# Padding of SBUF to multiples of 512 bytes, and another spread of the modulation row sums, in a two-block kernel on one core

## The chip, the core and the metric

The kernel runs on one core of a Trainium2 chip. Its time is the device time of one execution, in microseconds: 1427.51 us, the median of 3 runs (1427.47 to 1428.04). All data of a core pass through SBUF, a memory of 128 partitions in which a tile has a start address in bytes, the same in each partition. TensorE multiplies a stationary operand of 128 by 128 values, which a weight load brings in, with a moving operand of up to 512 columns that streams past it; both lie in SBUF.

## The reference

Two blocks are computed one after the other for 256 tokens of width 1024; the second also has 256 context tokens. All is float32. Cut to what matters here:

```python
# first block
x = x + 0.5 * swiglu(rmsnorm(x, ffn1_norm), gate, up, down)      # 1024 -> 2816 -> 1024
x = x + hybrid_mixer(rmsnorm(x, mix_norm), ...)                   # gated linear attention, conv
x = x + 0.5 * swiglu(rmsnorm(x, ffn2_norm), gate, up, down)
x = rmsnorm(x, final_norm)
# second block
h, hc = x + grid_pos_emb, ctx
mods   = split(silu(c)     @ w_ada + b_ada, 9)                    # w_ada: 1024 x 9216
mods_c = split(silu(c_ctx) @ w_ada + b_ada, 9)
h  = h  + 0.5 * mods[2]   * swiglu(modulate(rmsnorm(h),  mods[0],   mods[1]))
hc = hc + 0.5 * mods_c[2] * swiglu(modulate(rmsnorm(hc), mods_c[0], mods_c[1]))
h  = h + mods[5] * mixer(modulate(rmsnorm(h), mods[3], mods[4]), same of hc with mods_c)
h  = h + 0.5 * mods[8] * swiglu(modulate(rmsnorm(h), mods[6], mods[7]))
out = rmsnorm(h, g_final)
```

`modulate(x, shift, scale)` is `x * (1 + scale) + shift`.

## The kernel before, in words

**Products.** Each float32 product is made of three matmuls in the type fp32r. Every operand is held as a high and a low part: ScalarE writes the high part (`split_out`, line 66's activation, tiles `wh`, `XH`), VectorE the rest (line 69's subtraction, tiles `wl`, `XL`), and `mm3`, `mm3r`, `projT` and `projT2` add high by high, high by low and low by high into one PSUM tile `acc`. The matmul itself is line 79 for all of them.

**Stages.** The first block has a gated feed-forward layer for 256 tokens (`ffn2tok`: the gate-up projection in 11 steps of 4 units, then the down projection `d1` in 22 units), a mixer, and a second such layer (`ffn2tok` with `mid`, the preparation of the second block's inputs). The second block has a feed-forward layer for all 512 tokens (`ffn4tok`, two parts with a gate-up and a down projection each; a down projection runs twice, for either half of the 1024 outputs, over four tiles of 128 tokens), a mixer, and a last layer for 256 tokens.

**Units.** Weights come in units of 128 by 1024 values, 512 KB. SP's queue loads a unit into one of 4 buffers `raw`, ScalarE and VectorE split it into one of 5 pairs `wh`, `wl`. Units are handled in the order in which the code is written; each engine works its queue in order.

**Which operand is which.** In `proj_chunk` and in the down projections the weights stream (`wh`, `wl`, 512 columns of 4 bytes) past activations that are loaded as stationary operand: 128-column pieces of `XH` and `XL`, or of the tiles `S0` to `S17` that hold the hidden layer's high and low parts. In `projT2` the weights are stationary and `XH`, `XL` stream, 512 or 256 columns wide.

**Addresses.** Tiles are laid out one after the other, each rounded up to 32 bytes. What begins where, as the sizes of the tiles give it (bytes, and the rest after division by 512):

| tile | before: first byte | rest | after: first byte | rest |
|---|---|---|---|---|
| `ident` | 16512 | 128 | 16896 | 0 |
| `XH` | 18080 | 160 | 17408 | 0 |
| `XL` | 34464 | 160 | 33792 | 0 |
| `S0` | 91776 | 128 | 92672 | 0 |
| `S1` | 95904 | 160 | 97280 | 0 |
| `S2`, `S3` | 100032, 104128 | 192 | 101888, 105984 | 0 |
| `S4` to `S7` | 108256 + 4096 n | 224 | 110592 + 4096 n | 0 |
| `S8` to `S12` | 124672 + 4096 n | 256 | 127488 + 4096 n | 0 |
| `S13` to `S17` | 145184 + 4096 n | 288 | 148480 + 4096 n | 0 |
| `raw` (4), `wh` (5), `wl` (5) | 165664 + 4096 n | 288 | 168960 + 4096 n | 0 |

The rests of the `S` tiles differ because five of them once hold rows of 1032 values (4128 bytes; `CU` and `VH`), 32 bytes more than the others. Pieces of an operand lie at multiples of 512 bytes from its tile's start in nearly all products (exceptions: `VH`, with rows of 1032 bytes, and the second piece of `w_qk`, 1088 bytes in).

**Row sums.** `ada_gen` computes the modulation vectors `mods` outside TensorE: for each of 72 units of `w_ada` it loads the unit into a `raw` buffer and has VectorE multiply it with the broadcast silu(c) and sum each row (line 543; twice, for c and c_ctx, in the first 40 units, once in the last 32). It is a generator: `split` runs one more step of it after every `fill_every`-th unit of weights. `mid` runs it until 24 steps are done, `prep` to its end.

Of the kernel before, what the change touches and what calls it, by code (L numbers as in the profile page):

```python
# [9 lines left out]
F32 = mybir.dt.float32  # L10
F32R = mybir.dt.float32r
# [3 lines left out]
P = 128  # L15
D = 1024
FF = 2816
NF = FF // P
# [5 lines left out]
class Kern:  # L24
# [26 lines left out]
    def psum(self, tag, shape):  # L51
        return self.ps.tile(shape, F32, tag=tag, name=self.nm(tag), bufs=4)

    def salloc(self, shape, dt=F32):
        i = self.free_slots.pop(0)
        t = self.slots.tile(shape, dt, tag=f"S{i}", name=self.nm(f"S{i}"))
        self.slot_of[id(t)] = (i, t)
        return t

# [261 lines left out]
    def ffn2tok(self, Wgu, Wd, xts, rows, sink, after, skew=4, cols=False, first_by_tile=False, w0=(), fine=False, mid=None, ahead=None):  # L321


        hT = {}

        def dest(f):
            g = f // 4
            if g not in hT:
                hT[g] = (self.salloc([P, 4, 256], F32R), self.salloc([P, 4, 256], F32R))
            return hT[g] + (f % 4,)  # L330

        for c in range(1 if cols else 11):
            self.fill_every = 2 if self.filler is not None and 1 <= c < 10 else 0
            trs = []

            def sink_gu(t, ps, c=c, trs=trs):
                i = [a for a, _ in xts].index(t)
                r = rows.get(t)
                sil = self.t2([P, 256])
                h = self.t2([P, 256])  # L340
                if r is None:
                    self.act(sil, ps[:, :256], AF.Silu)
                    self.tt(h, ps[:, 256:], sil, ALU.mult)
                else:
                    self.act(sil, ps[:, :256], AF.Silu, scale=r)
                    self.stt(h, ps[:, 256:], r, sil, ALU.mult, ALU.mult)

                def later():
                    if i == 0:
                        trs.append(self.psum("tr", [P, 2, 256]))  # L350
                    tr = trs[0]
                    for f in range(2):
                        self.nc.tensor.transpose(tr[:, f, i * P:i * P + P], h[:, f * P:f * P + P], self.ident)
                    if i == 1:
                        hh, hl, sl = dest(2 * c)
                        self.split_out(hh[:, sl:sl + 2, :], hl[:, sl:sl + 2, :], tr)

                self.defer(later)

            self.proj_chunk(Wgu, 4 * c, xts, sink_gu, flush_at=2, last_by_tile=c == 0 and first_by_tile)  # L360
            if c == 0 and w0:
                for w in w0:
                    self.sfree(*w)
                self.held = 3
        if cols:
            toks = slice(xts[0][0] * P, xts[0][0] * P + 256)
            for f in range(2, NF):
                self.fill_every = 3 if self.filler is not None and f < 20 else 0
                ws = [self.unit(Wgu[2 * f + j]) for j in range(2)]
                pss = [self.psum("acc", [P, 256]) for _ in range(2)]  # L370
                self.projT2(pss, ws, toks)
                sil, h = self.t2([P, 256]), self.t2([P, 256])
                self.act(sil, pss[0], AF.Silu)
                self.tt(h, pss[1], sil, ALU.mult)
                hh, hl, sl = dest(f)
                self.split_out(hh[:, sl, :], hl[:, sl, :], h)
                if f == 2:
                    self.flush()
        if mid is not None:
            mid()  # L380
        ps = {}

        def step(f, i, t, d, w):
            wh, wl = w
            hh, hl, sl = dest(f)
            s = slice(d * 512, d * 512 + 512)
            if f == 0:
                ps[t, d] = self.psum("acc", [P, 512])
            a, b = hh[:, sl, i * P:i * P + P], hl[:, sl, i * P:i * P + P]
            self.mm3(ps[t, d], a, b, wh[:, s], wl[:, s], f == 0, f == NF - 1)  # L390

        for f in range(NF - skew):
            wh, wl = self.unit(Wd[f])
            hh, hl, sl = dest(f)
            groups = []
            for i, (t, _) in enumerate(xts):
                for d in range(2):
                    s = slice(d * 512, d * 512 + 512)
                    if f == 0:
                        ps[t, d] = self.psum("acc", [P, 512])  # L400
                    a, b = hh[:, sl, i * P:i * P + P], hl[:, sl, i * P:i * P + P]
                    groups.append((ps[t, d], a, b, wh[:, s], wl[:, s]))
            if fine and f == NF - skew - 1:
                self.mm3r(groups[:3], False, False)
                self.mm3r(groups[3:], False, True)
                sink(t, d, ps[t, d])
                continue
            for q in (groups[:2], groups[2:]) if f == 0 else (groups,):
                self.mm3r(q, f == 0, False)
            if f == 0:  # L410
                self.flush()
        ws = [self.unit(Wd[f]) for f in range(NF - skew, NF)]
        if ahead is not None:
            for g in range((NF - skew) // 4):
                self.sfree(*hT.pop(g))
            ahead()
        for i, (t, _) in enumerate(xts):
            for d in range(2):
                if fine and i == 1 and d == 1:
                    for q in (slice(0, 384), slice(384, 512)):  # L420
                        pq = self.psum("tr", [P, q.stop - q.start])
                        for f in range(NF - skew, NF):
                            (wh, wl), (hh, hl, sl) = ws[f - NF + skew], dest(f)
                            w = slice(512 + q.start, 512 + q.stop)
                            a, b = hh[:, sl, i * P:i * P + P], hl[:, sl, i * P:i * P + P]
                            self.mm3(pq, a, b, wh[:, w], wl[:, w], f == NF - skew, f == NF - 1)
                        sink(t, d, pq, q)
                        after(t, d, q)
                    continue
                for f in range(NF - skew, NF):  # L430
                    step(f, i, t, d, ws[f - NF + skew])
                sink(t, d, ps[t, d])
                after(t, d)
        for a, b in hT.values():
            self.sfree(a, b)

    def ffn4tok(self, Wgu, Wd, xts, sink, after, ws):

        u0 = 0
        for part, (f0, f1) in enumerate(((0, 12), (12, 22))):  # L440
# [15 lines left out]
            f = f0  # L456
# [12 lines left out]
            for f in range(f, f1):  # L469
# [2 lines left out]
                pss = [self.psum("acc", [P, 512]) for _ in range(2)]  # L472
                self.projT2(pss, ws, slice(0, 512))
                sink_gu(f, *pss)
            self.fill_every = 0
            nu = (f1 - f0) // 2
            for d in range(2):
                pss = {}

                def step(u, i, t, w):  # L480
# [623 lines left out]
    def run(self):  # L1104
        nc, A = self.nc, self.A
        x = {}
        for t in (2, 3):
            x[t] = self.xres.tile([P, D], F32, tag=f"x{t}", name=f"x{t}")
        self.ident = self.cpool.tile([P, P], F32, tag="ident", name="ident")
        make_identity(nc, self.ident)  # L1110
        g = {"f1": self.bc.tile([P, D], F32, tag="bc", name="bc_f1")}
        pre = []
# [5 lines left out]
        self.mhalf = self.cpool.tile([P, 4], F32, tag="mhalf", name="mhalf")  # L1118
        nc.gpsimd.memset(self.mhalf, -0.5)
        self.tri = self.cpool.tile([P, 2, P], F32, tag="tri", name="tri")  # L1120
        self.XH = self.cpool.tile([P, 8, 512], F32R, tag="XH", name="XH")
        self.XL = self.cpool.tile([P, 8, 512], F32R, tag="XL", name="XL")
        lat = (2, 3)

        def res_half(t, d, ps):
# [173 lines left out]
def body(tc, A, out):  # L1299
    with tc.tile_pool(name="const", bufs=1) as cpool, \  # L1300
            tc.tile_pool(name="xres", bufs=1) as xres, \
            tc.tile_pool(name="small", bufs=16) as small, \
            tc.tile_pool(name="tmp", bufs=6) as tmp, \
            tc.tile_pool(name="bc", bufs=4) as bc, \
            tc.tile_pool(name="rp", bufs=2) as rp, \
            tc.tile_pool(name="slots", bufs=1) as slots, \
            tc.tile_pool(name="raw", bufs=4) as raw, \
            tc.tile_pool(name="wsp", bufs=5) as wsp, \
            tc.tile_pool(name="dram", bufs=1, space=bass.MemoryType.DRAM) as dram, \
            tc.tile_pool(name="ps", bufs=1, space=bass.MemoryType.PSUM) as ps:  # L1310
        pools = dict(cpool=cpool, xres=xres, small=small, tmp=tmp, bc=bc, rp=rp, slots=slots, raw=raw, wsp=wsp, ps=ps)
        k = Kern(tc, A, out, pools)
        k.modd = dram.tile([112, P], F32, tag="modd", name="modd")
        k.mrow = dram.tile([36, 256], F32, tag="mrow", name="mrow")
        k.run()
# [129 lines left out]
```

## Time and profile before

| | us |
|---|---|
| median of 3 runs | 1427.51 |
| the profiled execution | 1426.11 |
| its span, first to last instruction | 1424.3 |
| TensorE busy in the span | 1404.2 (99%) |
| VectorE busy | 919.5 (65%) |
| ScalarE busy | 626.5 (44%) |

The page's sections are read from the top: busy time by engine, the span in 40 slices, DMA queues, the chain that ended last, groups of instructions. Matmuls overlap in the profile (the next begins before the last is out), so a group's mean duration is not its cost; the cost of one is the distance from one start to the next, and that is a stretch's length by its count of weight loads (one per matmul) in the view of busy time by stretch.

### The profile page before, as it was taken

The page shows a single profiled execution, that of the slowest core. Times are in us where ns is not written, and L with a number is a line of the kernel's source. Part 1 is how long each engine was busy: PE and PEld are TensorE (multiplying, and loading weights), DVE is VectorE, ACT ScalarE, POOL GpSimd, SP SyncE. Part 2 cuts the span into 40 slices and gives each one's busy share as a digit, 9 for nine tenths or more (in the row PEclk, how much of TensorE's full clock was granted, in tenths as well). Part 3 has the DMA queues.
Part 4 walks back from the last instruction along what each step waited for, and adds up shares of the span by engine and source line. Part 5 has one row for each costly group of instructions (what it writes and reads, how often), then busy time and mean ns, then how long its engine had stood idle before and what let it go on. Part 6 is the DMA issues. An engine that isn't in the chain of part 4 may idle for free. (4 is left out here: it accounts for less than half of the span.)

```text
span 1424.3 us, 18795 instructions
## 1 busy us (share of the span) xinstructions
PE 1404.2 (99%) x7222; PEld 1170.0 (82%) x7222; DVE 919.5 (65%) x1308; ACT 626.5 (44%) x914; POOL 29.3 (2%) x49
## 2 busy tenths in 40 slices
PE   7999999999999999999999999999999999999997
PEld 5888788778888898888888887888988887899986
DVE  5998556878988475542555446476886566655545
ACT  5445447464446442322122224343865455444442
POOL 0000000000000000000000001001010000000000
PEclk9999999999999999999999999999999999999999
DMA  8888646457887664643565442333335666465662
GB/s 278 307 269 275 205 136 204 134 166 259 290 275 254 203 210 132 195 147 102 191 209 178 147 148 94 115 104 129 102 104 187 198 192 206 142 197 179 184 207 69
DMA packets 73307, 260.71 MB, mean 183 GB/s; under 512 B 8172, under 2 KB 9216, under 8 KB 73216
## 3 DMA queue, kind: packets, MB, share of 16 engines
q1 hardware_dynamic: 72928, 259.11, 56.3%
q8 instruction: 57, 0.93, 0.3%
q10 hardware_dynamic: 288, 0.39, 0.1%
q14 instruction: 34, 0.28, 0.1%
HBM read 258.32 MB, written 1.14 MB: 182 GB/s over the span
## 5 line engine op out<-in xcount | busy, mean ns | idle before, releaser
L69 DVE TENSOR_TENSOR wl<-raw,wh 128x1024 fp32r<-128x1024 f32 (+1 forms) x381 | 459.0, 1212 | 330.3 <-ACT wh L66 326.7
L66 ACT ACTIVATE wh<-raw 128x1024 fp32r<-128x1024 f32 (+1 forms) x381 | 398.3, 1049 | 609.0 <-PE acc L79 457.9
L79 PE MATMUL acc<-wh,XH 128*128 128x512 f32 (+2 forms) x816 | 277.3, 398 | 0.4 <-ACT t L66 0.4
L79 PE MATMUL acc<-wh,XL 128*128 128x512 f32 (+2 forms) x816 | 273.4, 393 | 0.2 <-DVE XL L69 0.2
L79 PE MATMUL acc<-wl,XH 128*128 128x512 f32 (+2 forms) x816 | 272.4, 392 | 0.0
L79 PE MATMUL acc<-wh,S 128*128 128x512 f32 x872 | 237.1, 394 | 0.4 <-DVE t L72 0.4
L79 PE MATMUL acc<-XH,wh 128*128 128x512 f32 (+1 forms) x776 | 201.5, 339 | 0.0
L79 PE MATMUL acc<-XH,wl 128*128 128x512 f32 (+1 forms) x776 | 201.2, 339 | 0.0
L79 PE MATMUL acc<-XL,wh 128*128 128x512 f32 (+1 forms) x776 | 201.1, 339 | 0.0
L79 PEld LDWEIGHTS acc<-wh,S 128*128 128x128 f32 x872 | 162.8, 188 | 38.8 <-DVE t L72 1.1
L543 DVE SCALAR_TENSOR_TENSOR S<-raw,S 128x1024 f32<-128x1024 f32 x112 | 136.9, 1222 | 70.6 <-DMA raw<-in_w_ada 69.9
L79 PEld LDWEIGHTS acc<-wh,XL 128*128 128x128 f32 x816 | 152.2, 189 | 34.6 <-DVE XL L69 1.1
L79 PEld LDWEIGHTS acc<-wl,XH 128*128 128x128 f32 x816 | 152.0, 188 | 33.7 <-DVE wl L69 0.3
L79 PEld LDWEIGHTS acc<-wh,XH 128*128 128x128 f32 x816 | 151.7, 189 | 33.9 <-ACT t L66 0.6
L79 PEld LDWEIGHTS acc<-XL,wh 128*128 128x128 f32 x776 | 133.0, 188 | 17.5
L79 PEld LDWEIGHTS acc<-XH,wl 128*128 128x128 f32 x776 | 132.9, 188 | 17.5
L79 PEld LDWEIGHTS acc<-XH,wh 128*128 128x128 f32 x776 | 132.9, 188 | 17.5
L79 PE MATMUL acc<-wl,S 128*128 128x512 f32 x436 | 133.0, 393 | 0.0
L79 PEld LDWEIGHTS acc<-wl,S 128*128 128x128 f32 x436 | 81.9, 188 | 18.4
L66 ACT ACTIVATE S<-t 128x512 fp32r<-128x512 f32 (+2 forms) x58 | 31.4, 542 | 30.2 <-DVE t L69 30.2
L66 ACT ACTIVATE XH<-tr 128x512 fp32r<-128x512 f32 x44 | 26.0, 596 | 41.8 <-PE tr L152 41.3
L152 PE MATMUL tr<-ident,t 128*128 128x128 f32 x200 | 32.1, 285 | 10.4 <-DVE t L69 9.6
(165 smaller groups left out, 892.9 us busy)
## 6 DMA issues: line engine op xcount, KB each, us to landing
raw<-in_gu SPq DMA_DIRECT2D x176, 512.0 KB, 4.4
raw<-in_d SPq DMA_DIRECT2D x88, 512.0 KB, 4.3
raw<-in_w_ada SPq DMA_DIRECT2D x72, 512.0 KB, 4.5
raw<-in_w_in SPq DMA_DIRECT2D x68, 512.0 KB, 4.3
raw<-in_w_qk SPq DMA_DIRECT2D x16, 512.0 KB, 3.5
bc<-modd SPq DMA_DIRECT2D x10, 512.0 KB, 4.4
raw<-in_w_out SPq DMA_DIRECT2D x8, 512.0 KB, 3.5
raw<-in_w_b SPq DMA_DIRECT2D x8, 512.0 KB, 4.3
```

What stands on the lines that cost most here:

```text
L66: return self.nc.scalar.activation(out=out, in_=in_, func=func, **kw)
L69: return self.nc.vector.tensor_tensor(out=out, in0=a, in1=b, op=op)
L79: self.nc.tensor.matmul(out, l, r, start=start, stop=stop, **kw)
L152: self.nc.tensor.transpose(tr[:, j, :], src[:, j * P:(j + 1) * P], self.ident)
L543: nc.vector.scalar_tensor_tensor(out=junk, in0=raw, scalar=1.0, in1=cb[r], op0=ALU.mult, op1=ALU.mult, accum_out=mc[:, o:o + 1])
```

## The change

It pads pools so that every tile which is an operand of a product begins at a multiple of 512 bytes: 96 floats ahead of `ident`, `XH` and `XL` moved behind `ident`, 32 floats behind `tri`, 96 floats in the pool of the row factors, and the long `S` tiles rounded up from 4128 to 4608 bytes. The pads are never written or read. It also sets `fill_every` otherwise: in the first layer's gate-up every third unit instead of every second, in its down projection every third instead of none; in the four-tile layer's down projections every second unit instead of none, but for the very last one.

```diff
--- before.py
+++ after.py
@@ -51,9 +51,17 @@
     def psum(self, tag, shape):
         return self.ps.tile(shape, F32, tag=tag, name=self.nm(tag), bufs=4)
 
+    def pad(self, pool, n):
+
+        pool.tile([P, n], F32, tag=f"pad{n}", name=self.nm("pad"), bufs=1)
+
     def salloc(self, shape, dt=F32):
         i = self.free_slots.pop(0)
-        t = self.slots.tile(shape, dt, tag=f"S{i}", name=self.nm(f"S{i}"))
+        if len(shape) == 3 and shape[1] * shape[2] > D:
+            t = self.slots.tile([P, D + P], dt, tag=f"S{i}", name=self.nm(f"S{i}"))
+            t = t[:, :shape[1] * shape[2]].rearrange("p (a b) -> p a b", a=shape[1])
+        else:
+            t = self.slots.tile(shape, dt, tag=f"S{i}", name=self.nm(f"S{i}"))
         self.slot_of[id(t)] = (i, t)
         return t
 
@@ -330,7 +338,7 @@
             return hT[g] + (f % 4,)
 
         for c in range(1 if cols else 11):
-            self.fill_every = 2 if self.filler is not None and 1 <= c < 10 else 0
+            self.fill_every = (2 if mid else 3) if self.filler is not None and 1 <= c < 10 else 0
             trs = []
 
             def sink_gu(t, ps, c=c, trs=trs):
@@ -390,6 +398,7 @@
             self.mm3(ps[t, d], a, b, wh[:, s], wl[:, s], f == 0, f == NF - 1)
 
         for f in range(NF - skew):
+            self.fill_every = 3 if self.filler is not None and not mid and f < NF - skew - 2 else 0
             wh, wl = self.unit(Wd[f])
             hh, hl, sl = dest(f)
             groups = []
@@ -472,9 +481,9 @@
                 pss = [self.psum("acc", [P, 512]) for _ in range(2)]
                 self.projT2(pss, ws, slice(0, 512))
                 sink_gu(f, *pss)
-            self.fill_every = 0
             nu = (f1 - f0) // 2
             for d in range(2):
+                self.fill_every = 0 if part and d else 2
                 pss = {}
 
                 def step(u, i, t, w):
@@ -1106,7 +1115,10 @@
         x = {}
         for t in (2, 3):
             x[t] = self.xres.tile([P, D], F32, tag=f"x{t}", name=f"x{t}")
+        self.pad(self.cpool, 96)
         self.ident = self.cpool.tile([P, P], F32, tag="ident", name="ident")
+        self.XH = self.cpool.tile([P, 8, 512], F32R, tag="XH", name="XH")
+        self.XL = self.cpool.tile([P, 8, 512], F32R, tag="XL", name="XL")
         make_identity(nc, self.ident)
         g = {"f1": self.bc.tile([P, D], F32, tag="bc", name="bc_f1")}
         pre = []
@@ -1118,8 +1130,7 @@
         self.mhalf = self.cpool.tile([P, 4], F32, tag="mhalf", name="mhalf")
         nc.gpsimd.memset(self.mhalf, -0.5)
         self.tri = self.cpool.tile([P, 2, P], F32, tag="tri", name="tri")
-        self.XH = self.cpool.tile([P, 8, 512], F32R, tag="XH", name="XH")
-        self.XL = self.cpool.tile([P, 8, 512], F32R, tag="XL", name="XL")
+        self.pad(self.cpool, 32)
         lat = (2, 3)
 
         def res_half(t, d, ps):
@@ -1310,6 +1321,7 @@
             tc.tile_pool(name="ps", bufs=1, space=bass.MemoryType.PSUM) as ps:
         pools = dict(cpool=cpool, xres=xres, small=small, tmp=tmp, bc=bc, rp=rp, slots=slots, raw=raw, wsp=wsp, ps=ps)
         k = Kern(tc, A, out, pools)
+        k.pad(rp, 96)
         k.modd = dram.tile([112, P], F32, tag="modd", name="modd")
         k.mrow = dram.tile([36, 256], F32, tag="mrow", name="mrow")
         k.run()
```

Each engine issues the same instructions as before; some stand elsewhere. On VectorE, in the first layer's gate-up (`wl` is the low part of a unit, `mc` takes a row sum), there stands before:

```order
L543 SCALAR_TENSOR_TENSOR S_50_283,mc<-raw_384,S_48_277 128x1024
L543 SCALAR_TENSOR_TENSOR S_50_283,mc<-raw_384,S_49_280 128x1024
L69 TENSOR_TENSOR wl_403<-raw_400,wh_402 128x1024
L69 TENSOR_TENSOR wl_428<-raw_425,wh_427 128x1024
L543 SCALAR_TENSOR_TENSOR S_50_283,mc<-raw_431,S_48_277 128x1024
L543 SCALAR_TENSOR_TENSOR S_50_283,mc<-raw_431,S_49_280 128x1024
L69 TENSOR_TENSOR wl_458<-raw_455,wh_457 128x1024
```

and now:

```order
L552 SCALAR_TENSOR_TENSOR S_56_304,mc<-raw_383,S_54_298 128x1024
L80 SCALAR_TENSOR_TENSOR t_65_344<-acc_260,r_158,t_64_343 128x256
L552 SCALAR_TENSOR_TENSOR S_56_304,mc<-raw_383,S_55_301 128x1024
L80 SCALAR_TENSOR_TENSOR t_67_354<-acc_261,r_169,t_66_353 128x256
L77 TENSOR_TENSOR wl_402<-raw_399,wh_401 128x1024
L77 TENSOR_TENSOR wl_427<-raw_424,wh_426 128x1024
L77 TENSOR_TENSOR wl_453<-raw_450,wh_452 128x1024
L552 SCALAR_TENSOR_TENSOR S_56_304,mc<-raw_456,S_54_298 128x1024
L552 SCALAR_TENSOR_TENSOR S_56_304,mc<-raw_456,S_55_301 128x1024
```

Between two pairs of row sums there are now three subtractions of units instead of two. On SP's queue, at the beginning of the first down projection (`in_d` are its units), there stands before:

```order
L100 DMA raw_1231<-in_d 128x1024
L100 DMA raw_1262<-in_d 128x1024
L100 DMA raw_1280<-in_d 128x1024
L100 DMA raw_1298<-in_d 128x1024
L100 DMA raw_1316<-in_d 128x1024
```

and now:

```order
L108 DMA raw_1210<-in_d 128x1024
L108 DMA raw_1241<-in_d 128x1024
L108 DMA raw_1259<-in_d 128x1024
L549 DMA raw_1265<-in_w_ada 128x1024
L108 DMA raw_1281<-in_d 128x1024
L108 DMA raw_1299<-in_d 128x1024
L108 DMA raw_1317<-in_d 128x1024
L549 DMA raw_1323<-in_w_ada 128x1024
```

A unit of `w_ada` follows every third unit of the down projection, 5 in all, where there was none. On SP's queue at the beginning of the four-tile layer's first down projection there stands before:

```order
L540 DMA raw_5429<-in_w_ada 128x1024
L100 DMA raw_5432<-in_gu 128x1024
L540 DMA raw_5438<-in_w_ada 128x1024
L100 DMA raw_5497<-in_d 128x1024
L100 DMA raw_5531<-in_d 128x1024
L100 DMA raw_5561<-in_d 128x1024
```

and now:

```order
L549 DMA raw_5429<-in_w_ada 128x1024
L108 DMA raw_5432<-in_gu 128x1024
L549 DMA raw_5438<-in_w_ada 128x1024
L108 DMA raw_5497<-in_d 128x1024
L108 DMA raw_5531<-in_d 128x1024
L549 DMA raw_5537<-in_w_ada 128x1024
L108 DMA raw_5564<-in_d 128x1024
```

Here one follows every second unit, 6 in the first part, where there was none; the last units of `w_ada` are loaded that much earlier in the second gate-up that follows.

## Rows read from the trace of the kernel before

**Rows 1.** The page: span, engine line of TensorE, its granted clock in 40 slices.

```profile
span 1424.3 us, 18795 instructions
PE 1404.2 (99%) x7222; PEld 1170.0 (82%) x7222; DVE 919.5 (65%) x1308; ACT 626.5 (44%) x914; POOL 29.3 (2%) x49
PEclk9999999999999999999999999999999999999999
```

**Rows 2.** Waits of TensorE over the whole span; us in total, times, longest us.

```profile
PE tr L152 <- DVE t L69: 9.6, 3, 6.4
PE tr L152 <- DVE t L72: 0.8, 3, 0.4
PE acc L79 <- DVE t L72: 0.4, 1, 0.4
```

**Rows 3.** Groups of matmuls by form: moving operand first, then stationary; busy us, mean ns.

```profile
L79 PE MATMUL acc<-wh,XH 128*128 128x512 f32 x784 | 271.3, 402 | 0.4 <-ACT t L66 0.4
L79 PE MATMUL acc<-wh,S 128*128 128x512 f32 x872 | 237.1, 394 | 0.4 <-DVE t L72 0.4
L79 PE MATMUL acc<-wl,S 128*128 128x512 f32 x436 | 133.0, 393 | 0.0
L79 PE MATMUL acc<-XH,wh 128*128 128x512 f32 x392 | 123.8, 395 | 0.0
L79 PE MATMUL acc<-XH,wh 128*128 128x256 f32 x384 | 77.7, 282 | 0.0
L79 PE MATMUL acc<-XH,S 128*128 128x256 f32 x128 | 20.8, 282 | 0.0
L79 PE MATMUL tr<-S,S 128*128 128x258 f32 x112 | 22.0, 290 | 0.0
```

**Rows 4.** Busy time by stretch, four stretches of down projections; head row gives columns.

```profile
core 0: us, PE busy (x) PEld busy (x) DVE busy (x) ACT busy (x) POOL busy (x), PEclk, DMA share, GB/s
657.72:668.62 10.90, 10.90 (x49) 9.01 (x48) 2.45 (x2) 2.11 (x3) 0.00 (x0) 1.00 0.32 96
668.62:679.82 11.20, 11.20 (x49) 9.00 (x48) 6.08 (x8) 1.69 (x2) 0.00 (x0) 1.00 0.30 94
154.46:166.35 11.89, 11.89 (x53) 9.76 (x52) 5.20 (x5) 4.79 (x5) 0.00 (x0) 1.00 0.68 187
460.34:483.67 23.33, 23.33 (x101) 18.74 (x100) 11.20 (x11) 9.07 (x9) 0.00 (x0) 1.00 0.70 211
```

**Rows 5.** The same view, three stretches of gate-up projections (PEld count is weight loads).

```profile
58.22:68.94 10.72, 10.72 (x47) 8.63 (x46) 10.22 (x14) 4.83 (x7) 0.00 (x0) 1.00 0.87 267
580.09:646.55 66.46, 66.46 (x287) 53.89 (x286) 29.64 (x38) 18.35 (x26) 0.00 (x0) 1.00 0.48 154
1246.31:1354.49 108.18, 108.18 (x914) 108.18 (x913) 58.14 (x77) 51.18 (x77) 0.00 (x0) 1.00 0.61 188
```

**Rows 6.** The same view, the stretches into and out of which row sums move.

```profile
20.00:134.00 114.00, 114.00 (x509) 92.02 (x509) 100.95 (x138) 56.68 (x74) 1.41 (x1) 1.00 0.83 276
142.00:194.00 52.00, 51.55 (x225) 41.41 (x224) 25.35 (x24) 21.23 (x23) 0.42 (x2) 1.00 0.64 189
646.60:713.10 66.50, 66.50 (x289) 53.80 (x288) 31.46 (x39) 14.52 (x15) 0.00 (x0) 1.00 0.49 152
713.30:825.00 111.70, 111.70 (x480) 89.87 (x479) 54.78 (x72) 29.35 (x38) 0.00 (x0) 1.00 0.53 173
```

**Rows 7.** Waits: ScalarE in 20 to 134 us; TensorE in 142 to 146 us.

```profile
ACT wh L66 <- DMA raw<-in_gu: 53.2, 31, 4.8
PEld acc L79 <- DVE t L72: 1.1, 2, 0.9
```

**Rows 8.** The page's groups of the splits and of the row sums.

```profile
L69 DVE TENSOR_TENSOR wl<-raw,wh 128x1024 fp32r<-128x1024 f32 (+1 forms) x381 | 459.0, 1212 | 330.3 <-ACT wh L66 326.7
L66 ACT ACTIVATE wh<-raw 128x1024 fp32r<-128x1024 f32 (+1 forms) x381 | 398.3, 1049 | 609.0 <-PE acc L79 457.9
L543 DVE SCALAR_TENSOR_TENSOR S<-raw,S 128x1024 f32<-128x1024 f32 x112 | 136.9, 1222 | 70.6 <-DMA raw<-in_w_ada 69.9
```

## The prediction

> **What bounds the kernel now.** I read the page's head first: TensorE is busy for 1404.2 of 1424.3 us and holds 2.4 GHz in every slice [rows 1]. Then TensorE's waits: 9.6 us for VectorE at three transposes and little else [rows 2]. So TensorE's own pace is the time; what any other engine gains is worth nothing as long as it keeps ahead.
>
> So the question is what one matmul costs, and I took the forms next [rows 3]. Three matmuls make a product and have like counts, so one row stands for three: 784 of `wh` past `XH` (2352 in all), 392 of `XH` past `wh` (1176), 872 + 436 = 1308 with an `S` tile as stationary operand, 48 that stream an `S` tile; together 4884 of 512 columns. Besides, about 1560 have 256 or so columns (384 in each of three forms, then 128 and 112 in the rows, the rest smaller). 512 columns at 2.4 GHz are 213.3 ns.
>
> Last I read the distance between starts, as length by weight loads, in stretches that hold one kind of matmul and in which TensorE is busy throughout [rows 4, 5]. The first two stretches of [rows 4] are the proof on which I build: 48 matmuls each, same weights, same shapes, one behind the other; only the stationary tiles differ. In the first they are `S13`, `S14`, `S16`, `S17`, in the second `S8` to `S11` (I followed the built program's tiles along the trace). 10.90 us / 48 = 227.1 ns against 11.20 / 48 = 233.3 ns. By the table of addresses both `wh` and `S13` leave a rest of 288, `S8` leaves 256. The third stretch (`S5` to `S7`, rest 224) has 11.89 / 52 = 228.7 ns, the fourth (`S8` to `S12`, another layer) 23.33 / 100 = 233.3. So the distance follows the difference of the two rests: 0 gives 227.1, 64 gives 228.7, 32 gives 233.3. Where `wh` and `XH` meet, 128 apart, it is 10.72 / 46 = 233.0 with `wh` streaming and 66.46 / 286 = 232.4 with `XH` streaming [rows 5]. VectorE and DMA do not explain it: at 233.0 VectorE is busy 95% and DMA 87%, at 233.3 they are 54% and 30%, at 228.7 they are 44% and 68%.
>
> **The change part by part.** *The padding.* It issues nothing and takes nothing away; it makes every difference of rests 0 (but for `VH` and the second piece of `w_qk`). I price each matmul at the only row with difference 0, 227.1 ns:
> - 2352 + 48 with `wh` or an `S` tile past `XH`, `XL`: between 233.0 and 232.4 now; I take 232.7, so 5.6 ns each, 13.4 us.
> - 1176 with `XH`, `XL` past `wh`, `wl`: 5.3 ns each, 6.2 us.
> - 1308 with an `S` tile: counted in the built program 422 at rest 256 (6.2 ns, 2.6 us), 352 at rest 224 (1.6 ns, 0.6 us), 412 at rest 288 (nothing), 122 at others (priced as rest 256: 0.8 us). 4.0 us.
>
> That is 23.6 us. The 1560 narrower ones cost 108.18 / 913 = 118.5 ns [rows 5]; none with difference 0 is long enough to be read. Their floor is 256 columns at 2.4 GHz, 106.7 ns, or 18 us less in all; above, I bound them by the 0.4% by which like stretches differ (233.0 against 232.4), 1 us more. I take the nearest row, their own: 0.
>
> VectorE and ScalarE also read padded tiles. A split's two operations have all operands at rest 288 now, a row sum has 288, 192 and 128 or 160; they take 1212 and 1222 ns on VectorE for the same 1024 columns [rows 8]. So I expect no change there; were it 1% either way, it would be under 5 us on an engine that is 35% idle.
>
> *Row sums out of the first gate-up.* 18 units of `w_ada` become 12, so 6 units with two sums of 1.22 us [rows 8], 14.6 us of VectorE, and 6 loads of 512 KB go. VectorE is busy there 100.95 of 114 us and DMA moves 276 GB/s [rows 6]; ScalarE waits 53.2 us for units [rows 7], yet TensorE has no wait: the transfers are hidden. With 509 matmuls 5.9 ns shorter, TensorE needs 111 us; VectorE falls to 86, DMA to 28.3 MB / 111 us = 255 GB/s. Gain now: nothing. It buys cover: without it the faster TensorE would ask for 283 GB/s, and if DMA held at 276 the padding would lose its 2.8 us here. The one stall at the seam, weight loads waiting 1.1 us for VectorE [rows 7], may shorten with VectorE less behind; I take 0.4 us off.
>
> *Row sums into the first down projection.* 5 units: 12.2 us of VectorE on 25.35 in 52 us, so 37.5 of 51 [rows 6]; DMA 9.8 + 2.6 MB in 51 us = 243 GB/s, under the 276 that the stretch before sustains. Each is queued on SP and in `raw` ahead of the next `in_d` unit, for which the splits, then TensorE, wait; both engines have room. Cost 0; if the cover went, one unit's passage, 512 KB at 276 GB/s = 1.9 us, five times, 9.5 us.
>
> *Row sums into the four-tile down projections.* 6 units with one sum each in the first part (the steps after the 40th): 7.3 us on VectorE's 31.46 in 66.5 us; six where SP's queue held only `in_d` [rows 6]. As many leave the second gate-up (54.78 of 111.7 us) and `prep`. Cost 0, by the same cover.
>
> Sum: 23.6 + 0.4 = 24 us. The profiled execution took 1426.1 us with its span of 1424.3, so 1402 us; the median of the runs is 1.4 us above it, which gives 1403.5. I write 1403.
>
> **A rule against the change.** The two stretches above, 227.1 and 233.3 ns, differ in nothing but an address [rows 4]. The Trainium skill, "TensorE: Matmul & The Clock Gate", section "Step-by-step: what each phase is for", says that TensorE has separate SBUF read ports for the streaming and the stationary operand and that "Loading the next tile's weights doesn't steal SBUF read bandwidth from the running matmul". By it no address would matter and the time would stay 1427.5; by the rows it is 1403. The measurement decides.
>
> **The rivals.**
> *The start counts too, not the difference alone.* A rest of 288 is 32 past a multiple of 64, and no row has both operands at multiples of 512. 227.1 is 13.8 ns above the bare 213.3. If all of that went, 4884 x 13.8 = 67 us more and 18 us on the narrow ones: 1318. If a third went, 1375. For it: something holds each matmul above its columns. Against it: streams at rest 288, 160 and as `S` tiles give about the same 233, so no start has been seen to matter by itself. By the same page, section "Back-to-back issue gap", a matmul of 512 columns follows the last after 512/2.4 + 2.5 = 215.8 ns; as an estimate this would be 55 us below the forecast, and no run here shows that distance.
>
> *Only part follows.* The 227.1 row has an `S` tile as stationary operand; pairs of `XH` and `wh` have never been seen at difference 0. If one of these two kinds stays, the gain is 10 to 18 us: 1410 to 1418.
>
> *The padding does nothing* (the `S13` tiles are fast for another reason, as their place): 1427. Against it: the same tiles are slow against other partners, and the differences order the rows.
>
> *Slower: operands in step collide.* With everything at rest 0, both reads of TensorE and those of VectorE and ScalarE start alike. If that is a bad case, as 32 apart is worse than 64, the price is at each 512-column matmul: at 240 ns, as far above the worst row as that is above the best, 4884 x (240 - 232.2) = 38 us, 1465. It decides from a mean of 232.2 on. Against it: difference 0 is the best row there is.
>
> **How the numbers follow.** Forecast, 1396 to 1411: 62%. More by the start: 18%, mostly near 1375 to 1395. Only part: 10%. Nothing: 5%. Slower: 5%. What can be told from no change in this kernel is about 0.2%, 3 us; the first three cases are faster by more, so faster 0.90, same 0.05, slower 0.05. The range leaves out the far end of the first rival below (some 9%) and the last two above: 1365 to 1417.
>
> **What would show it.** In the profile after, the two stretches of 48 in the four-tile down projection are both at 227 ns; the gate-up stretches fall from 233.0 and 232.4 to 227; the narrow ones stay at 118.5. In 20 to 131 us VectorE's share falls from 89% to about 78% and DMA's rate to 255 GB/s; in the first down projection VectorE rises to some 73% and TensorE has no new wait. I am wrong if distances stay apart by tile, if they fall well below 227, or if TensorE waits for splits behind a row sum.

## The result, and the profile after

The changed kernel takes 1412.34 us (median of 4 runs, 1411.32 to 1415.59), the kernel before 1427.49 on the same chip: a ratio of 0.9897, with a 95% interval of 0.988 to 0.9914. It is faster by 15.2 us; the forecast was faster by 24.5, to 1403. The time lies in the range, 9.3 us from the forecast. It is 1.3 us outside the band of 1396 to 1411 that the forecast itself was given, and inside the band of the rival "only part follows", whose mechanism the stretches below refute. The profiled execution took 1411.32 us.

First the page of the changed kernel: its span, the row of TensorE, TensorE's busy tenths in 40 slices and the granted clock in the same slices. They answer to [rows 1].

```profile
span 1409.5 us, 18797 instructions
PE 1385.3 (98%) x7222; PEld 1172.0 (83%) x7222; DVE 918.6 (65%) x1308; ACT 627.8 (45%) x914; POOL 30.4 (2%) x49
PE   7999899999999999999999999999999999999997
PEclk9999999999999999999999999999999999999999
```

TensorE is busy for 18.9 us less (1404.2 before), but the span lost only 14.8. The fifth slice, 141 to 176 us, shows an 8 between nines, where before has a 9: TensorE has got an idle stretch that it did not have. The list of waits over the whole span names it (us in total, times, longest us); the second row answers to a wait of 0.4 us in [rows 2], the first is as it was.

```profile
PE tr L160 <- DVE t L77: 9.7, 3, 6.8
PE acc L87 <- DVE t L80: 3.5, 1, 3.5
```

Next the view of busy time by stretch. The stretches hold the same matmuls as those of [rows 4, 5] (found by following the built program's order along the trace; of the fourth, the last 239 of its 286 distances), and after them the two stretches of 20 to 134 and 142 to 194 us of [rows 6].

```profile
core 0: us, PE busy (x) PEld busy (x) DVE busy (x) ACT busy (x) POOL busy (x), PEclk, DMA share, GB/s
651.68:662.56 10.88, 10.88 (x50) 9.01 (x48) 3.60 (x4) 2.12 (x3) 0.00 (x0) 1.00 0.52 180
662.56:673.44 10.88, 10.88 (x50) 9.01 (x48) 6.84 (x10) 1.47 (x2) 0.00 (x0) 1.00 0.44 140
57.25:67.93 10.68, 10.68 (x48) 8.77 (x47) 9.08 (x12) 4.59 (x6) 0.00 (x0) 1.00 0.76 280
586.39:640.59 54.20, 54.20 (x241) 44.86 (x240) 27.41 (x36) 15.46 (x22) 0.00 (x0) 1.00 0.58 177
1230.88:1340.40 109.52, 109.52 (x916) 109.52 (x914) 58.11 (x77) 51.32 (x78) 0.00 (x0) 1.00 0.61 188
20.00:134.00 114.00, 114.00 (x521) 94.34 (x520) 91.06 (x120) 61.29 (x79) 1.41 (x1) 1.00 0.80 268
142.00:194.00 52.00, 48.92 (x211) 40.40 (x212) 32.23 (x36) 19.07 (x19) 0.42 (x2) 0.97 0.67 215
```

The two stretches of 48 matmuls, 227.1 and 233.3 ns each in [rows 4], now take 10.88 us both: 226.7 ns. Gate-up with `wh` streaming fell from 233.0 to 10.68 / 47 = 227.2 ns, with `XH` streaming from 232.4 to 54.20 us for 239 distances between starts, 226.8 ns. The last layer's 256-column matmuls went the other way: 109.52 us for 912 distances is 120.1 ns, against 118.8 before, counted the same way (108.18 us for 911 distances; divided by weight loads, as in the prediction, it was 118.5). And from 142 to 194 us TensorE is idle for 3.1 us and its clock is 0.97, where it was idle for 0.45 at 1.00 [rows 6].

Here is that stretch close up, which [rows 7] showed only as a small wait: TensorE, VectorE and SP's DMA queue where the first gate-up passes into the first down projection. Each is a timeline (start, us busy, engine, line, operation, tiles, count, and in brackets the idle time ahead and what ended it). TensorE after the change:

```profile
141.16 0.39 PE L87 MATMUL acc<-wl,S 128*128 128x512 f32 x1
145.08 0.74 PE L87 MATMUL acc<-wh,S 128*128 128x512 f32 x2 [3.54 <-DVE t L80]
...
146.27 3.64 PE L87 MATMUL acc<-wh,S 128*128 128x512 f32 x8
```

VectorE after the change:

```profile
139.34 0.68 DVE L77 TENSOR_TENSOR S<-tr,S 128x512 fp32r<-128x512 f32 x1
139.94 0.47 DVE L80 SCALAR_TENSOR_TENSOR t<-acc,r,t 128x256 f32<-128x256 f32 x1
143.39 1.23 DVE L552 SCALAR_TENSOR_TENSOR S<-raw,S 128x1024 f32<-128x1024 f32 x1 [2.98 <-DMA raw<-in_w_ada]
...
144.54 0.48 DVE L80 SCALAR_TENSOR_TENSOR t<-acc,r,t 128x256 f32<-128x256 f32 x1
```

SP's queue after the change:

```profile
124.13 3.04 SPq L108 DMA_DIRECT2D raw<-in_d  x3
129.37 0.33 SPq L549 DMA_DIRECT2D raw<-in_w_ada  x1
131.89 5.62 SPq L108 DMA_DIRECT2D raw<-in_d  x3
138.31 0.33 SPq L549 DMA_DIRECT2D raw<-in_w_ada  x1
```

VectorE has two accumulators of the last gate-up step to drain, that is, to read out of PSUM so that their buffers come free (line 80, `t<-acc`). Between them the change has put a row sum (line 552), whose unit SP issued only at 138.31 us, behind loads of `in_d` that had waited for `raw` buffers, and which was there at about 143.4. VectorE works its queue in order. ScalarE had done its part of the second accumulator by 140.0 us (139.52 + 0.48 in its timeline), yet VectorE stood idle for 2.98 us, did the sum, and drained only at 144.54; for the buffer that this drain frees, TensorE's next matmul waited 3.54 us. Then the eight `wh` past `S` from 146.27 us on take 3.64 us, where the row sums alone, below, show 2.11 for the same eight. Before, VectorE has the two drains back to back:

```profile
143.09 0.68 DVE L69 TENSOR_TENSOR S<-tr,S 128x512 fp32r<-128x512 f32 x1
143.69 0.87 DVE L72 SCALAR_TENSOR_TENSOR t<-acc,r,t 128x256 f32<-128x256 f32 x2
144.48 1.22 DVE L69 TENSOR_TENSOR wl<-raw,wh 128x1024 fp32r<-128x1024 f32 x1
```

### The profile page after: what moved, and what is told of

Same layout as the page of the kernel before. It is cut to its first block, busy times and chain, and to the rows that moved or that the text cites. A ratio compares the mean times of both kernels' runs of the same rounds, so it can differ in the third digit from the quotient of the medians.

```text
span 1409.5 us, 18797 instructions
## 1 busy us (share of the span) xinstructions
PE 1385.3 (98%) x7222; PEld 1172.0 (83%) x7222; DVE 918.6 (65%) x1308; ACT 627.8 (45%) x914; POOL 30.4 (2%) x49
## 5 line engine op out<-in xcount | busy, mean ns | idle before, releaser
L87 PE MATMUL acc<-wh,XH 128*128 128x512 f32 (+2 forms) x816 | 274.0, 394 | 0.3 <-ACT t L74 0.3
L87 PE MATMUL acc<-wh,XL 128*128 128x512 f32 (+2 forms) x816 | 269.7, 388 | 0.2 <-DVE XL L77 0.2
L87 PE MATMUL acc<-wl,XH 128*128 128x512 f32 (+2 forms) x816 | 268.4, 387 | 0.0
L87 PEld LDWEIGHTS acc<-XH,wh 128*128 128x128 f32 x776 | 133.6, 190 | 15.5
```

The source lines that it names most:

```text
L87: self.nc.tensor.matmul(out, l, r, start=start, stop=stop, **kw)
```

## The experiments

The theory with which they began: the distance between matmuls goes by the difference of the two operands' starts, and the rest of the change costs what the seam shows. Rivals: a row sum anywhere in the down projection costs time; the starts themselves count too.

### The padding alone

Against the changed kernel (`...` marks what is left out, here and below):

```diff
-            self.fill_every = (2 if mid else 3) if self.filler is not None and 1 <= c < 10 else 0
+            self.fill_every = 2 if self.filler is not None and 1 <= c < 10 else 0
...
-            self.fill_every = 3 if self.filler is not None and not mid and f < NF - skew - 2 else 0
...
+            self.fill_every = 0
             nu = (f1 - f0) // 2
             for d in range(2):
-                self.fill_every = 0 if part and d else 2
```

> The padding without the new spread of the row sums (fill_every as before). Theory: the padding is worth 4884 matmuls of 512 columns at about 227 ns instead of 232.2 (24.6 us by the changed kernel's trace) less 1500 narrower ones at 120.0 instead of 118.6 ns (2 us), and the rest of the measured change is a loss at the seam into the first down projection, which this kernel does not have: 1405 us. If the first gate-up then waits for its units (6 loads per step instead of 5.33), up to 3 us of it go: 1405 to 1408, with waits of TensorE in 20 to 140 us. Rival: the spread is needed, and without it the faster TensorE runs into transfers: 1412 us or more.

Measured: 1410.1 us (1408.8 to 1415.0), before on the same chip 1427.88; ratio 0.9884, 0.9869 to 0.99. By its interval it can't be told from the changed kernel: the padding carries the whole gain, and the new spread of the row sums adds nothing as it stands. It lies between the 1405 to 1408 expected and the 1412 of the rival. TensorE's waits in 40 to 142 us, where before has 0.3 us of weight loads and no matmul waiting:

```profile
PEld acc L87 <- DVE wl L77: 4.8, 6, 1.5
PE acc L87 <- DVE wl L77: 2.0, 3, 1.0
```

The stretch 20 to 134 us of this kernel:

```profile
20.00:134.00 114.00, 111.73 (x502) 90.25 (x501) 100.34 (x138) 54.99 (x69) 1.39 (x1) 1.00 0.82 273
```

With as many row sums in the gate-up as before, TensorE does 502 matmuls there, fewer than the 509 of before [rows 6], and weight loads wait for units that VectorE has not split. DMA moves 273 GB/s against 276 before. Here the faster matmuls gain nothing: they wait for units, as the prediction said of a kernel without the cover.

### The row sums alone

The change to `fill_every` as in the diff, no pads, the tiles where they were.

> The new spread of the row sums without any padding. Theory: the wait of 3.5 us at the start of the first down projection comes from a row sum that stands between the two drains of the last gate-up step on VectorE and waits for its load; it is there without the padding too, and eight matmuls at half clock follow it: 1427.5 + 4 to 6 = 1431 to 1434 us, with TensorE waiting for line 72's drain at about 143 us. Rival: the wait only comes because TensorE is faster with the padding: 1427 us, no such wait.

Measured: 1427.36 us (11 runs, 1426.22 to 1431.34) against 1427.88; ratio 1.0, 0.9991 to 1.0009. So no change, and the expected loss of some us is not in the medians. The mechanism is in the trace all the same. VectorE at the seam:

```profile
141.40 0.47 DVE L72 SCALAR_TENSOR_TENSOR t<-acc,r,t 128x256 f32<-128x256 f32 x1
144.90 1.23 DVE L544 SCALAR_TENSOR_TENSOR S<-raw,S 128x1024 f32<-128x1024 f32 x1 [3.04 <-DMA raw<-in_w_ada]
...
146.05 0.48 DVE L72 SCALAR_TENSOR_TENSOR t<-acc,r,t 128x256 f32<-128x256 f32 x1
```

and TensorE behind it:

```profile
146.59 0.73 PE L79 MATMUL acc<-wh,S 128*128 128x512 f32 x2 [2.50 <-DVE t L72]
...
147.75 2.11 PE L79 MATMUL acc<-wh,S 128*128 128x512 f32 x8
```

The same row sum stands between the same two drains and TensorE waits 2.50 us, without any padding. (With the padding TensorE begins its last matmul ahead of the wait 2.5 us earlier, at 141.16 us instead of 143.70, and the sum starts 1.5 us earlier, 143.39 instead of 144.90: so the wait is some 1 us longer.) Its next eight matmuls take 2.11 us, not 3.64. So the wait comes from the row sums; what follows it in the changed kernel, the slow eight, does not come with every such wait. The profiled execution of this kernel, 1428.05 us, is 1.94 us longer than that of before, about what the wait costs. Why the medians show none of it stays open: the runs scatter by as much.

### The row sums later in the first down projection

All of the change, but for the one line by which the first down projection takes its row sums: from its seventh step on, every second unit, so that none stands at the seam.

```diff
-            self.fill_every = 3 if self.filler is not None and not mid and f < NF - skew - 2 else 0
+            self.fill_every = 2 if self.filler is not None and not mid and 6 <= f < NF - skew - 2 else 0
```

> The changed kernel, but the row sums in the first down projection begin at its 7th unit (every second unit from there) instead of its 3rd; no row sum stands between the two drains of the last gate-up step on VectorE any more. Theory: the 3.5 us wait goes and with it eight matmuls at half clock (8 x 200 ns = 1.6 us): 1412.3 - 5.2 = 1407 us. Rival: the load of the units themselves is late there (SP's queue waits for buffers), and another wait of the same size takes its place: 1412 us.

Measured: 1405.74 us (1405.70 to 1405.98), ratio 0.9844, 0.9831 to 0.9858. The stretch of 8.5 us at the seam in four kernels. Before:

```profile
141.00:149.50 8.50, 8.05 (x37) 6.13 (x36) 5.93 (x9) 5.69 (x8) 0.00 (x0) 1.00 0.85 262
```

The changed kernel:

```profile
141.00:149.50 8.50, 4.96 (x18) 3.67 (x17) 5.65 (x8) 1.54 (x2) 0.00 (x0) 0.81 0.54 189
```

The row sums alone:

```profile
141.00:149.50 8.50, 6.00 (x29) 4.57 (x28) 5.46 (x9) 3.08 (x5) 0.00 (x0) 1.00 0.58 179
```

The changed kernel with later row sums:

```profile
141.00:149.50 8.50, 8.50 (x41) 7.03 (x40) 6.36 (x7) 3.92 (x5) 0.00 (x0) 1.00 0.45 153
```

TensorE does 18 matmuls in the changed kernel and 41 in this one; the granted clock is 0.81 there and 1.00 here. By the medians, moving the row sums of five units (two sums each) is worth 1412.34 - 1405.74 = 6.6 us (the runs of before beside them have 1427.49 and 1427.88), and the runs lie within 0.3 us instead of 4.3. The slower clock is hardly an accident of the profiled execution: over whole runs the granted clock is 0.996 or 0.997 in all four of the changed kernel and 0.998 in all four of this one; the row sums alone have 0.998 or 0.999 in ten of eleven runs, and 0.995 in the one that took 1431.34 us. In the profiles the stretch from the 584th to the 830th matmul, which holds the seam, is 3.47 us longer than before in the changed kernel and 1.95 shorter here: 5.4 us. That a row sum in the down projection costs time wherever it stands is refuted: the same ten stand here, a few steps later, and TensorE does not wait.

### Start distances by the difference of the starts

A kernel that computes nothing of the reference: blocks of 48 matmuls of `n` columns, the moving operand `rm` bytes and the stationary `rs` bytes past a multiple of 512, with VectorE at rest and DMA all but so.

```python
for i in range(48):
    m = rm // 4 + 512 * (i // 2 % 4)
    s = rs // 4 + 128 * (i % 8)
    nc.tensor.matmul(acc[:, :n], S[:, s:s + 128], M[:, m:m + n], start=i == 0, stop=i == 47)
```

> Nothing of the layer is computed: blocks of 48 fp32r matmuls, stationary and moving operand from two tiles that begin at multiples of 512 bytes, for 512 and 256 columns. In 16 blocks the stationary operand begins 0, 32, ... 480 bytes off; in 4 both begin 32, 64, 160 or 288 off; in 4 the moving one alone 32, 64, 160 or 448. Theory: the distance follows the difference alone (stationary less moving, over 512): with 512 columns 226.7 ns at 0, about 229 at 448 and 64, 233 at 480 and 32, 234 at 416, 232.5 at 128 and 384; 226.7 for all blocks with both moved. With 256 columns 120.0 at 0 and for both moved, 118 to 119 at 64, 96 and 128. Rival: the start itself counts: blocks with both moved differ from difference 0 by some ns.

The view of busy time by stretch; the rows are blocks of 512 columns in the order of time: stationary operand 0, 32, 96, 192 and 256 bytes further than the moving one, then both operands 32 and both 160 bytes off, then two blocks of 256 columns, difference 0 and 64.

```profile
29.82:40.70 10.88, 10.88 (x49) 9.01 (x48) 0.00 (x0) 0.18 (x1) 0.00 (x0) 1.00 0.00 0
40.71:51.89 11.18, 11.18 (x49) 9.02 (x48) 0.00 (x0) 0.18 (x1) 0.00 (x0) 1.00 0.00 0
...
63.10:74.33 11.23, 11.23 (x49) 9.03 (x48) 0.00 (x0) 0.18 (x1) 0.00 (x0) 1.00 0.00 0
...
96.70:107.68 10.98, 10.98 (x49) 9.02 (x48) 0.00 (x0) 0.18 (x1) 0.00 (x0) 1.00 0.00 0
...
118.89:129.77 10.88, 10.88 (x49) 9.01 (x48) 0.00 (x0) 0.18 (x1) 0.00 (x0) 1.00 0.00 0
...
207.96:218.87 10.91, 10.91 (x49) 9.01 (x48) 0.00 (x0) 0.18 (x1) 0.00 (x0) 1.00 0.00 0
...
229.78:240.71 10.93, 10.93 (x49) 9.01 (x48) 0.00 (x0) 0.18 (x1) 0.00 (x0) 1.00 0.01 1
...
296.25:302.00 5.75, 5.75 (x50) 5.75 (x48) 0.00 (x0) 0.18 (x1) 0.00 (x0) 1.00 0.00 0
...
307.67:313.31 5.64, 5.64 (x50) 5.64 (x49) 0.00 (x0) 0.18 (x1) 0.00 (x0) 1.00 0.02 4
```

With 512 columns the first row, the difference 0, has 10.88 / 48 = 226.7 ns; 32 bytes give 232.9, 96 the most, 234.0, and 192 give 228.8 (from first to last start in the trace 226.7, 233.2, 234.2 and 229.0; 64, 128, 160 and 224, not shown, lie at 232.5 to 233.4 by this count). At 256 bytes it is 226.7 again: the pattern repeats after 256 bytes, not 512. Both operands 32 off give 227.3, both 160 off 227.7: the difference rules, the start by itself hardly counts, and the rival that all would fall well below 227 is refuted. With 256 columns it is the other way: the starts in a block of difference 0 are 119.8 ns apart, with 64 they are 117.8 (from first to last start; the rows divide to 119.8 and 117.5).

### The 256-column matmuls on a grid of starts

The same kernel with 24 matmuls of 256 columns for each pair of starts in steps of 32 bytes, and four differences finer than 32 bytes with 512 columns.

> Nothing of the layer is computed: 256 blocks of 24 fp32r matmuls of 256 columns, every start of the moving and of the stationary operand from 0 to 480 bytes past a multiple of 512 in steps of 32, and four blocks of 512 columns with the stationary operand 4, 8, 16 and 48 bytes off. The run before showed one of its 256-column blocks at 113.7 ns (moving 448, stationary 0), against 120 at difference 0 and 117.8 at the same difference of 64 with the moving operand at 0. Theory: for 256 columns the start of the moving operand counts beside the difference, so blocks of equal difference split; some cell is at 113 to 114 ns and none under it. Rival: the difference alone counts and 113.7 was an accident of that block's place: all cells of a diagonal are alike, 117.8 for a difference of 64. Differences below 32 bytes: between 226.7 and 233.

In ns between starts (first to last of a block), medians of the 32 cells of equal difference (bytes over a multiple of 256), and the finer differences:

```
256 columns, difference    0      32     64     96     128    160    192    224
ns                         119.6  118.3  117.8  117.3  118.4  120.1  117.8  117.9
512 columns, difference    4      8      16     48
ns                         232.3  230.7  233.3  233.3
```

Three cells of the grid, all of difference 64: starts 0 and 64, 64 and 128, and 128 and 192 (24 matmuls, 23 distances).

```profile
47.96:50.67 2.71, 2.71 (x25) 2.71 (x24) 0.00 (x0) 0.18 (x1) 0.00 (x0) 1.00 0.03 6
144.49:147.20 2.71, 2.71 (x26) 2.71 (x24) 0.00 (x0) 0.18 (x1) 0.00 (x0) 1.00 0.00 0
241.16:243.78 2.62, 2.62 (x25) 2.62 (x24) 0.00 (x0) 0.18 (x1) 0.00 (x0) 1.00 0.00 0
```

Two have 2.71 / 23 = 117.8 ns, the third 2.62 / 23 = 113.9, with the same difference. Three more cells of the 32 are like it (moving and stationary operand at 224 and 32, 384 and 192, 480 and 32), and one pair of starts that was fast in the kernel before this one, the moving operand at 448 and the stationary one at 0, has 118.0 ns here where it had 113.7. So the narrow matmuls have a second, faster pace that the difference does not decide, nor the two starts by themselves. What sets it stays open. Nor is the diagonal of 96 uniform: four of its cells have 120.1.

### The last layer's operands 64 and 96 bytes earlier

The kernel with later row sums, and `XH` and `XL` moved 64 bytes (in a second kernel 96) down for the last layer alone, so that its 256-column matmuls have that difference.

```diff
+    def place_X(self, early):
+        o = P - early // 4
+        self.XH, self.XL = [t[:, o:o + 4096].rearrange("p (k t) -> p k t", k=8) for t in self.Xt]
...
             if t == 2 and d == 0:
+                self.place_X(64)
```

> The kernel with the later row sums, and in the last layer (256 columns past stationary weights) XH and XL begin 64 bytes earlier, so the stationary operand is 64 bytes ahead of the moving one, over 256. Theory: 911 + 48 matmuls there cost 117.8 ns instead of 120.0, as most cells of that diagonal in the grid, 2.1 us: 1403.6 us; if the stream falls into the other state that the grid showed in four cells, 113.3 ns, 6.4 us: 1399.3. The first step of that layer, 48 matmuls of 512 columns, loses 0.1 us. Rival: with two tiles XH and XL and weights that change every six matmuls no steady state forms, 120 as before: 1405.7.

> The same with XH and XL 96 bytes earlier in the last layer. Theory: 117.2 ns instead of 120.0 by the grid, in every cell of that diagonal: 959 x 2.8 = 2.7 us, less 0.3 us for the 48 matmuls of 512 columns at 233.4: 1403.3 us. Rival: no steady state, 1405.7 to 1406.

Measured: 64 bytes 1401.62 us (1398.69 to 1403.11), ratio 0.9813, 0.9798 to 0.9828; 96 bytes 1403.94 (1403.48 to 1405.9), ratio 0.9832, 0.9818 to 0.9845; both against 1428.44 on one chip. For 64 bytes 1403.6 was expected, or 1399.3 in the faster pace; for 96, 1403.3. The last layer's 912 distances, 64 bytes:

```profile
1228.73:1332.18 103.45, 103.45 (x915) 103.45 (x914) 58.12 (x77) 51.34 (x78) 0.00 (x0) 1.00 0.64 196
```

and 96 bytes:

```profile
1227.97:1335.06 107.09, 107.09 (x915) 107.09 (x914) 58.10 (x77) 51.28 (x78) 0.00 (x0) 1.00 0.62 191
```

That is 113.4 and 117.4 ns, where the changed kernel has 120.1. At 96 the pace is that of the grid (117.3). At 64 the profiled execution has the faster pace, yet it took 1403.11 us, only 2.7 less than the profiled execution with later row sums, where the last layer alone gives 6.1 back. Part of the rest is this wait in the second gate-up, at two places where a row sum stands between two drains; the kernel with later row sums has the sums there too, and its profile lists no such wait:

```profile
PE tr L365 <- DVE t L84: 1.7, 2, 1.1
```

The version with 64 bytes, at 1401.6 us, beats both kernels. Beside the later row sums with `XH` where it was (ratio 0.9831 to 0.9858) the interval for 64 bytes lies apart, that for 96 overlaps.

## Why the prediction was right and wrong

**The matmuls of 512 columns: right.** Predicted 23.6 us from two stretches of 48 matmuls. From the start times of both traces (means of the distances under 260 ns), 2352 matmuls fell by 5.3 ns, 1176 by 6.0, 1308 by 3.5 and 48 by 3.8: 24.3 us. Both pairs of 48 meet at 226.7 ns as foretold, and the blocks with an idle VectorE and no DMA show that the address alone does it. One reading was wrong without harm: I took the difference without its sign. The 228.7 ns belong to a stationary operand 64 bytes behind the moving one, which is 192 over a multiple of 256 (229.0 in the blocks); 64 bytes ahead of it has 233.4. The Trainium skill, "TensorE: Matmul & The Clock Gate", section "Step-by-step: what each phase is for", says that loading the next weights takes no read bandwidth from the running matmul, since its two operands have separate ports. If nothing else set the distance, no row of the blocks could differ from the next; 10.88 against 11.23 us for 48 matmuls differ, and the measurement decides. What inside the chip makes the difference count was not tried.

**The matmuls of 256 columns: a term missed.** I priced them at their own row, 118.5 ns, with 1 us more as the bound above. At difference 0 they are dearer, 120.1 ns; 1.3 ns on each of the 1152 with `wh` or `wl` and the 248 with `S` as stationary operand are about 2 us. No row of before had that difference (`XH` and `wh` were 128 apart, for which the blocks give 118.5), and I bounded it by how far like stretches agree (233.0 against 232.4 ns, which is 0.26% and not the 0.4% that I wrote). That is not a bound on a case that was never seen. What failed here is the step that took a price from another difference.

**Row sums into the first down projection: the step that failed.** I wrote "Each is queued on SP and in `raw` ahead of the next `in_d` unit ... both engines have room. Cost 0". VectorE rose from 25.35 us to 32.23 of the 52 in the stretch, 62% where I had put some 73%: it was not short of time. What I left out is the order on it: the sum was queued between two drains from PSUM, and it waited for its own load. The engine's share doesn't tell that; the question is what stands behind an instruction that can wait. I had named what waits behind the load on SP (the splits), not what waits behind the sum on VectorE (a drain, and TensorE's accumulator). The wait grew from 0.45 us to 3.54, and the granted clock in the stretch fell to 0.81. Together 5.4 us in the profiles and 6.6 in the medians, by the kernel with later row sums. My bound for this edit, 9.5 us if the cover went, held; my value for it did not.

**Row sums out of the first gate-up: right in kind.** Cost nothing, gain nothing by itself, but cover for the padding. VectorE fell to 91.06 us in 114 (80%; 78 foretold), DMA to 268 GB/s (255 foretold), and TensorE has no wait there, with 521 matmuls instead of 509. ScalarE still waits there for units, as in [rows 7]:

```profile
ACT wh L74 <- DMA raw<-in_gu: 39.2, 23, 4.7
```

The row is of the changed kernel's waits in 20 to 134 us (in total, times, longest): 39.2 us instead of 53.2, and none of it reaches TensorE. Without the cover the padding loses it: 502 matmuls in the padding alone. I had put that at 2.8 us; the first gate-up of that kernel is 4.3 us longer than with later row sums. But the 0.4 us that I took off the seam became a loss, for the reason above.

**Row sums into the four-tile down projections: right.** The stretch from the 3204th to the 3972nd matmul, which holds them, is 3.98 us shorter than before, with no new wait of TensorE; with the padding alone, where these sums are not there, it is 3.86 us shorter.

The sum with what was measured: 24.3 gained, about 2 lost on the narrow matmuls, makes some 22, and the kernel without the seam's wait gained 22.1 (1427.88 - 1405.74). That this comes near the 24 of the forecast is in part luck: the long matmuls gave 0.7 us more than their price, and the narrow ones took 2 that had no price. The changed kernel gives 6.6 back, which leaves 15.5; beside its own runs of before it gained 15.2.

**The rivals.** That only part of the pairs follows and that the padding does nothing fell with the stretches after. That the start counts too fell with the blocks in which both operands are shifted alike, and with the floor: 226.7 ns is the lowest of the blocks, so the 13.8 ns above the bare columns did not go. That operands in step collide fell with the difference 0 as the best 512-column row, but the narrow matmuls show a small price of that kind, where I had put it on the long ones (the mean of my rows for those is 231.9 ns, not the 232.2 in that rival's sum, so its 38 us should read 39). The new wait of TensorE that I named as a sign of error, "if TensorE waits for splits behind a row sum", came as a wait for a drain behind a row sum.

## What to carry to other kernels

Where TensorE is the bound, read the distance between matmul starts by operand pair, and put operands so that a pair's starts differ by a multiple of 256 bytes if the matmul is long; measure short ones apart, since their order is another. Before filler work goes onto an engine with idle time, look at what is queued behind it on that engine: a row sum that waited 2.98 us for its load held up the drain behind it on an engine that was busy 62% of the stretch. And put such work where no accumulator is about to be freed: the row sums of the same five units cost 6.6 us at the seam of two stages, and a few steps later TensorE did not wait for them.

## What the runs showed of the hardware beyond that

- The distance between 512-column matmuls depends on the difference of the operands' starts with a period of 256 bytes: 226.7 ns at 0 (to 227.7 with both operands shifted alike), 228.8 to 234.4 at other multiples of 32, and 230.7 to 233.3 even at 4, 8 and 16 bytes.
- At 256 columns the order is another, 119.5 to 120.2 ns at 0 and 117.3 in most cells of 96, and there is a second pace of 113.4 to 114.3 that appeared with some blocks of difference 64 and not with others.
- TensorE stood still 3.54 us in the changed kernel, and the 8.5 us that hold this wait have a mean granted clock of 0.81: of the eight 512-column matmuls that begin 1.2 us after the wait has ended, the second to the eighth start 426 to 427 ns apart, which is 512 columns at the lower level, 1.2 GHz. After a wait of 2.50 us at the same place, in the kernel with the row sums alone, the clock stayed at 1.00 in the profiled execution.
